# One product of the SSD scan moved from POOL to VectorE, in a hybrid SSD and attention layer

## The chip, the cores and the metric

The kernel runs on one core of a Trainium2 chip, as one program with one launch. The metric is the device time of one execution in microseconds, and a kernel's time is the median over its runs. The profile is one more execution, taken by the hardware profiler. Engine names are those of the profile: PE is TensorE, DVE is VectorE, ACT is ScalarE, POOL is GpSimd and SP is SyncE, which here only issues DMAs.

## The reference

One layer works on 1024 prompt tokens and on 8 streams of 16 tokens, 1152 tokens in all, with a model width of 1024. One input projection feeds two branches, a Mamba-2 scan (the SSD branch: 32 heads of 64 in 8 groups, state width 128) and a forgetting attention (16 heads of 64). The branches are gated, projected back, merged and normalized. What matters here is the chunked scan, cut to its core:

```python
acum = jnp.cumsum(dtc * A, axis=2)
seg = acum[:, :, :, None] - acum[:, :, None]
decay = jnp.exp(jnp.where(causal, seg, -jnp.inf))
cb = jnp.einsum('bclgn,bcsgn->bclsg', Cc, Bc)
m = cb[..., None] * decay * dtc[:, :, None]
y_diag = jnp.einsum('bclsgr,bcsgrp->bclgrp', m, xc)
...
y_off = jnp.einsum('blgn,bgrpn->blgrp', c_c, s_in) * jnp.exp(acum_c)[..., None]
```

For each head and each block of tokens there are two products: `y_diag`, the masked and decayed matrix C·B times the inputs of the block, and `y_off`, C times the state that enters the block, times the decay exp(acum) of each token. The kernel applies that second decay to C ahead of the matmul.

## The kernel before, in words

Everything is fp32. A dense projection splits its inputs and weights into a high and a low part and takes three matmul passes (lines 244 to 246, in `passes`). A weight tile gives 128 output columns for all 1152 tokens, in three column chunks c = 0, 1, 2 of 384 tokens (in chunk 2, 256 tokens are of the prompt and 128 of the streams). Each chunk is 24 matmuls into one PSUM bank, and these products have two banks (tag `d`). So PE starts a chunk's 24 matmuls only when the chunk two before it has been read out of its bank. Who reads it out depends on the column:

- columns of x, B and C (`conv_dense`): ACT copies the bank (L539, in chunk 2 also L545) and starts the convolution (L540). DVE adds the three other taps (L551), ACT takes a tanh (L552) and DVE finishes with L553. The result for C is the tile `acc…c`, `Cf` in the scan.
- columns of the gate z (`silu_dense`): ACT takes a tanh (L569), DVE reads the bank again and multiplies (L570).

Weights are split into parts by ACT and POOL (L223, L224) or, where they have a scale, by ACT and DVE (L226, L227).

The scan runs per group g of four heads. While PE works on the six weight tiles of group g+1 (`group_dense`), a generator `group(g)` is advanced a step at a time by the clock of `passes` (the class `Flow`), so that the scan's small operations are put between the dense matmuls. For each chunk of three token blocks it does this:

- `rows` has SP load, for each head, the running sum acum of the chunk, broadcast to 128 partitions, into a tile `ce`.
- `transp` has PE transpose x and B; DVE multiplies by dt (L612), POOL by the decay to the block's end (L614).
- `cbt` computes C·B and masks it into `cbm` (DVE, L646 and L649).
- `decay`, called twice with two heads each, forms for each head three blocks of exponents `m` from `ce` (DVE, L687), then ACT takes exp of `ce` in place (L689) and of `m` (L690), DVE multiplies `m` by `cbm` (L691), and POOL multiplies `ce` by C in place (L692), 384 columns wide in chunks 0 and 1 and 256 in chunk 2.
- `states` carries the state from block to block (POOL L667, DVE L668).
- `readout` of a chunk, which comes in the next chunk or at the end, has PE multiply with `m` (L708) and with `ce` (L712). DVE adds the skip term (L721), POOL multiplies by the gate (L724), and ACT squares (L727, L729) for the norm, summed by POOL (L730).
- for the streams, POOL decays the states (L751) and DVE adds the updates (L767).

Each engine works through its own queue in order. For this part of the kernel, the order in the queue is not that of the text: the framework's planner orders the operations at compile time, by priority (the order of the text) among those whose inputs its own model has ready. So operations of a later step can stand far ahead of their place in the code. Later parts (attention, merging) have an order written by hand.

Of the kernel before, what the change touches and what calls it, by code (L numbers as in the profile page):

```python
# [15 lines left out]
ALU = mybir.AluOpType  # L16
# [133 lines left out]
def trunk_step(ctx: ExitStack, tc: tile.TileContext, I, O):  # L150
    nc = tc.nc
    ve, ac, po, te, sy = nc.vector, nc.scalar, nc.gpsimd, nc.tensor, nc.sync
# [438 lines left out]
    def group(g, r):  # L591

        sp = lazy["spb"]
        xs, z, Bf, Cf = [r["x0"], r["x1"]], [r["z0"], r["z1"]], r["b"], r["c"]
# [84 lines left out]
        def decay(c, i):  # L679
            w = CW if c < 2 else 256  # L680
            for e in range(2):
                h = 4 * g + 2 * i + e
                m = sp.tile([P, 3, P], F32, tag="m", name=f"m{c}_{h}", bufs=4)
                ce = ces[c, 2 * i + e]
                for j in range(3):
                    b = 3 * c + j
                    ve.tensor_scalar(m[:, j, :], ce[:, j * P:(j + 1) * P], nacum[:, b, h:h + 1], 0.0,  # L687
                                     ALU.add, ALU.min)
                ac.activation(ce[:, :w], ce[:, :w], AF.Exp)  # L689
                ac.activation(m[:], m[:], AF.Exp)  # L690
                ve.tensor_tensor(m[:], m[:], cbms[c][:], ALU.mult)  # L691
                po.tensor_tensor(ce[:, :w], ce[:, :w], Cf[c][:, :w], ALU.mult)  # L692
                mm[c, 2 * i + e] = m

        def readout(c):
# [76 lines left out]
        for c in range(NCH):  # L772
            for j in range(3):
                transp(3 * c + j)
                yield Y
                if c and j == 0:
                    readout(c - 1)
                    yield 2 * Y
            cbt(c)
            yield Y  # L780
            if c == 2:
                stk = stack()
                sample_out()
                yield Y
            decay(c, 0)
            yield Y
            states(c)
            if c == 2:
                for q in range(4):
                    sample_decay(q)  # L790
            yield Y
            decay(c, 1)
            if c < 2:
                for i in range(2):
                    rows(c + 1, i)
            yield Y
# [563 lines left out]
    for c in range(NCH):  # L1360
# [27 lines left out]
        for j in range(3):  # L1388
            b, w = 3 * c + j, width[j]
# [107 lines left out]
```

## Time and profile before

| | us |
|---|---|
| three runs | 2066.13, 2066.86, 2064.82 (median 2066.13) |
| profiled execution | 2064.78 |
| its span, from first to last instruction | 2062.9 |
| scan with the projection of the columns it needs | about 184 to 985 of the span |
| one group in that stage | about 100 |
| busy in the whole span: PE, DVE, ACT, POOL | 2028.5, 1376.8, 820.1, 594.6 |

The lines of a profile that follow below have these forms. A line of the timeline has the start in the span, the duration, the engine, the line of the code, the operation, the tile written and the tiles read, their shapes and how many instructions follow on each other (x3); in brackets stands the idle time of the engine before it, and what ended that. A line of the waits says who waited for whom, with the sum, the number of waits and the longest. A line of the windows says how long an engine was busy in a stretch. A line of one source line has the smallest, the median and the largest duration in ns.

### The profile page before, as it was taken

How to read it: one execution, taken by the hardware profiler on the slowest of the kernel's cores; microseconds unless marked ns; L12 is line 12 of the kernel's file. 1: busy time of each engine (PE TensorE's matmuls, PEld its weight loads, DVE VectorE, ACT ScalarE, POOL GpSimd, SP SyncE). 2: the span in 40 equal slices, each digit the busy share in tenths (PEclk: the TensorE clock that was granted, in tenths of full speed). 3: DMA queues.
4: the chain of work that ended last, by engine and by line, in shares of the span. 5: the costliest groups of instructions: out<-in, count | busy, mean ns of one | idle time of the engine just before them, and what ended most of it. 6: DMA issues, size and time to landing. Idle time of an engine off the chain costs nothing.

```text
span 2062.9 us, 36057 instructions
## 1 busy us (share of the span) xinstructions
PE 2028.5 (98%) x14263; PEld 1868.2 (91%) x14263; DVE 1376.8 (67%) x2278; ACT 820.1 (40%) x1647; POOL 594.6 (29%) x775
## 2 busy tenths in 40 slices
PE   9999999999999999999999999999999999999998
PEld 7899989899998999999988888888889899999987
DVE  4145788887878787874487787777777774173355
ACT  5124444444434344443445554545455452122210
POOL 0013565555556564644100100110010002114400
PEclk9999999999999999999999999999999999999999
DMA  6412242423232323242556566556656584154222
GB/s 221 161 65 90 71 134 71 126 77 119 81 126 78 118 91 114 87 134 91 185 196 194 186 206 207 188 179 199 212 184 202 186 301 147 41 171 152 82 106 92
DMA packets 123624, 292.49 MB, mean 142 GB/s; under 512 B 18632, under 2 KB 74944, under 8 KB 113216
## 3 DMA queue, kind: packets, MB, share of 16 engines
q1 hardware_dynamic: 110912, 208.93, 31.7%
q10 hardware_dynamic: 12544, 81.27, 11.4%
q8 instruction: 112, 1.84, 0.4%
q14 instruction: 56, 0.46, 0.1%
HBM read 233.64 MB, written 56.51 MB: 141 GB/s over the span
## 4 chain that ended last, share of the span: by engine, by line
PE 67%; DVE 20%; ACT 5%; DMA 4%; issue 2%; POOL 1%; ACTq 0%; DVEq 0%; SPq 0%; POOLq 0%
PE d L244 14%; PE d L246 13%; PE d L245 13%; PE s L914 3%; DVE m L687 2%; PE o L989 2%; PE v L333 2%; PE v L334 2%; PE v L332 2%; PE dq L245 2%; PE dq L244 2%; PE dq L246 2%; PE out L1381 2%; PE out L1380 2%; PE out L1382 2%
## 5 line engine op out<-in xcount | busy, mean ns | idle before, releaser
L244 PE MATMUL d<-xh,wh 128*128 128x384 f32 x2112 | 740.9, 351 | 21.3 <-DVE z3z L570 2.1
L246 PE MATMUL d<-xh,wl 128*128 128x384 f32 x2112 | 708.7, 336 | 0.0
L245 PE MATMUL d<-xl,wh 128*128 128x384 f32 x2112 | 707.8, 335 | 0.0
L244 PEld LDWEIGHTS d<-xh,wh 128*128 128x128 f32 x2112 | 397.2, 188 | 54.6 <-issue 17.7
L245 PEld LDWEIGHTS d<-xl,wh 128*128 128x128 f32 x2112 | 397.6, 188 | 0.8
L246 PEld LDWEIGHTS d<-xh,wl 128*128 128x128 f32 x2112 | 396.7, 188 | 0.0
L224 POOL TENSOR_TENSOR wl<-wr,wh 128x1024 fp32r<-128x1024 f32 x52 | 125.5, 2413 | 348.8 <-ACT wh L223 348.8
L687 DVE TENSOR_SCALAR m<-ce,nacum 128x128 f32<-128x128 f32 x288 | 141.6, 553 | 5.9 <-PE y L708 5.9
L223 ACT CAST wh<-wr 128x1024 fp32r<-128x1024 f32 x64 | 67.0, 1047 | 194.9 <-PE d L245 157.1
L919 ACT ACTIVATE st<-s,ckt 128x256 f32<-128x256 f32 (+1 forms) x320 | 115.1, 466 | 20.1 <-PE s L914 14.8
L923 POOL TENSOR_TENSOR st<-st,mask_bf 128x256 f32<-128x256 f32 x64 | 48.3, 775 | 196.8 <-ACT st L919 196.7
L979 ACT ACTIVATE st<-st 128x1024 f32<-128x1024 f32 x80 | 83.1, 1062 | 43.6 <-DVE st L974 41.0
L227 DVE SCALAR_TENSOR_TENSOR wl<-wr,wh 128x1024 fp32r<-128x1024 f32 x50 | 62.2, 1243 | 32.5 <-ACT wh L226 32.1
L614 POOL TENSOR_TENSOR wx<-xdt,wdt 128x256 f32<-128x256 f32 x72 | 56.8, 790 | 50.9 <-DVE xdt L612 50.9
L989 PE MATMUL o<-st,vt 128*64 128x256 f32 (+1 forms) x640 | 69.5, 363 | 1.6 <-ACT st L979 1.2
L989 PEld LDWEIGHTS o<-st,vt 128*64 128x64 f32 x640 | 42.8, 137 | 28.4 <-ACT st L979 5.1
L245 PE MATMUL d<-yb1l,wh 128*128 128x384 f32 x192 | 64.2, 334 | 0.0
L244 PE MATMUL d<-yb1h,wh 128*128 128x384 f32 x192 | 64.2, 334 | 0.0
L246 PE MATMUL d<-yb0h,wl 128*128 128x384 f32 x192 | 64.2, 334 | 0.0
L246 PE MATMUL d<-yb1h,wl 128*128 128x384 f32 x192 | 64.2, 334 | 0.0
L245 PE MATMUL d<-yb0l,wh 128*128 128x384 f32 x192 | 64.2, 334 | 0.0
L244 PE MATMUL d<-yb0h,wh 128*128 128x384 f32 x192 | 64.2, 334 | 0.0
(635 smaller groups left out, 4093.9 us busy)
## 6 DMA issues: line engine op xcount, KB each, us to landing
wr<-in_wt SPq DMA_DIRECT2D x88, 512.0 KB
kc<-in_cache_k ACTq DMA_DIRECT2D x32, 1024.0 KB
vc<-in_cache_v ACTq DMA_DIRECT2D x32, 1024.0 KB
ce<-ac_d SPq DMA_DIRECT2D x96, 192.0 KB
wr<-in_wbr SPq DMA_DIRECT2D x24, 512.0 KB
gate_d<-gate SPq DMA_DIRECT2D x48, 192.0 KB
sb<-cs_d ACTq DMA_DIRECT2D x16, 576.0 KB
yr<-ym_d SPq DMA_DIRECT2D x16, 576.0 KB
```

Of the source, the lines that this page charges most:

```text
L223: ac.copy(hi[:, :cols], raw[:, :cols])
L224: lazy.get("sub", po).tensor_tensor(lo[:, :cols], raw[:, :cols], hi[:, :cols].bitcast(F32), ALU.subtract)
L227: ve.scalar_tensor_tensor(lo[:, :cols], raw[:, :cols], scale, hi[:, :cols].bitcast(F32), ALU.mult, ALU.subtract)
L244: te.matmul(out, wh, xh, start=(k == 0), stop=False)
L245: te.matmul(out, wh, xl, start=False, stop=False)
L246: te.matmul(out, wl, xh, start=False, stop=(k == n - 1))
L614: po.tensor_tensor(wx[b][:], xdt[b][:], wdt[:, b, hs][:, :, None].to_broadcast([P, 4, 64]), ALU.mult)
L687: ve.tensor_scalar(m[:, j, :], ce[:, j * P:(j + 1) * P], nacum[:, b, h:h + 1], 0.0, ALU.add, ALU.min)
L914: te.matmul(ps2[:, e, 256 * x + q0:256 * x + 256], kk[hr, ks], qq[hr, qs], start=(at == 0), stop=(at == 2))
L919: ac.activation(S[j][:, e, kb, q0:], ps2[:, e, 256 * x + q0:256 * x + 256], AF.Identity, bias=ckt[:, kb, 2 * hp + e:2 * hp + e + 1])
L979: ac.activation(w, w, AF.Exp, scale=-1.0)
L989: te.matmul(o[64 * e:64 * e + 64, 256 * at + q0:256 * at + 256], vt[:, kb, 64 * e:64 * e + 64], S[j][:, e, kb, q0:256], start=(kb == 0), s ...
```

## The change

The product of the exponentiated row with C moves from POOL to DVE. In the text it stands behind the product of `m` with the mask, as before.

```diff
                 ac.activation(ce[:, :w], ce[:, :w], AF.Exp)
                 ac.activation(m[:], m[:], AF.Exp)
                 ve.tensor_tensor(m[:], m[:], cbms[c][:], ALU.mult)
-                po.tensor_tensor(ce[:, :w], ce[:, :w], Cf[c][:, :w], ALU.mult)
+                ve.tensor_tensor(ce[:, :w], ce[:, :w], Cf[c][:, :w], ALU.mult)
                 mm[c, 2 * i + e] = m
```

It is executed 96 times: 8 groups, 3 chunks, 4 heads.

## The prediction

> **What bounds the kernel now.** I read the page's first lines, then the busy times in the stage of the scan, then PE's waits in that stage. The first shows PE as the bound of the whole; the second, for PE, DVE, ACT and POOL in that order, leaves PE 805 − 783.0 = 22 us idle between 180 and 985 us; the third says for whom.
>
> ```profile
> span 2062.9 us, 36057 instructions
> PE 2028.5 (98%) x14263; PEld 1868.2 (91%) x14263; DVE 1376.8 (67%) x2278; ACT 820.1 (40%) x1647; POOL 594.6 (29%) x775
> ```
> ```profile
> 180.00:985.00 805.00, 783.03 (x5303) 740.50 (x5302) 630.09 (x1152) 341.87 (x742) 440.55 (x592) 1.00 0.33 103
> ```
> ```profile
> PE d L244 <- DVE z4z L570: 1.8, 2, 1.5
> PE d L244 <- ACT raw4x L545: 1.0, 1, 1.0
> PE d L244 <- ACT raw4c L545: 0.4, 1, 0.4
> ```
>
> The waits are the rows of one group (4); the other groups have rows like them. PE stands still in three places of a group and a little in a fourth, each time for a bank of the dense product that ACT or DVE has not read out yet. So the change can gain at most those 22 us, and it can lose whatever it adds in front of these read-outs. POOL and DVE have idle time, and neither is a bound by its sum. What decides is who stands in front of whom in DVE's and ACT's queues.
>
> The three places, PE's rows first, then ACT's, then DVE's, in the timeline:
>
> ```profile
> 502.32 0.44 PE L244 MATMUL d<-xh,wh 128*128 128x384 f32 x1 [0.38 <-ACT raw3c L545]
> ```
> ```profile
> 535.62 0.45 PE L244 MATMUL d<-xh,wh 128*128 128x384 f32 x1 [1.02 <-ACT raw4x L545]
> ```
> ```profile
> 563.71 0.44 PE L244 MATMUL d<-xh,wh 128*128 128x384 f32 x1 [1.54 <-DVE z4z L570]
> ```
> ```profile
> 499.81 0.53 ACT L552 ACTIVATE raw3c<-acc3c 128x384 f32<-128x384 f32 x1 [3.07 <-DVE acc3c L551]
> ...
> 533.11 0.53 ACT L552 ACTIVATE raw4x<-acc4x 128x384 f32<-128x384 f32 x1 [1.98 <-DVE acc4x L551]
> ...
> 562.17 0.52 ACT L690 ACTIVATE m<-m 128x384 f32<-128x384 f32 x1 [0.61 <-DVE m L687]
> 562.60 0.47 ACT L569 ACTIVATE z4z<-d 128x384 f32<-128x384 f32 x1
> ```
> ```profile
> 494.13 1.26 DVE L687 TENSOR_SCALAR m<-ce,nacum 128x128 f32<-128x128 f32 x2
> 495.31 4.10 DVE L551 SCALAR_TENSOR_TENSOR acc3c<-raw3c,cw,acc3c 128x384 f32<-128x384 f32 x3
> ...
> 522.92 0.61 DVE L721 SCALAR_TENSOR_TENSOR yt<-acc3x,dcol,y 128x384 f32<-128x384 f32 x1
> 523.45 2.24 DVE L687 TENSOR_SCALAR m<-ce,nacum 128x128 f32<-128x128 f32 x3
> ...
> 526.13 3.79 DVE L687 TENSOR_SCALAR m<-ce,nacum 128x128 f32<-128x128 f32 x7
> 529.84 3.18 DVE L551 SCALAR_TENSOR_TENSOR acc4x<-raw4x,cw,acc4x 128x384 f32<-128x384 f32 x3
> ...
> 554.79 0.48 DVE L687 TENSOR_SCALAR m<-ce,nacum 128x128 f32<-128x128 f32 x2
> ...
> 555.71 2.32 DVE L687 TENSOR_SCALAR m<-ce,nacum 128x128 f32<-128x128 f32 x5
> ...
> 558.48 3.60 DVE L687 TENSOR_SCALAR m<-ce,nacum 128x128 f32<-128x128 f32 x5
> ```
>
> I call them the places C, X and Z. At C (502.3) and X (535.6), PE waits for ACT's copy L545; that stands in ACT's queue behind the tanh L552, and the tanh waits for DVE's three L551, which come late. At Z (563.7) the gate's bank is read by ACT L569, which stands behind an exp L690 that waits for DVE's L687. So in all three the late one is DVE, with L687 and L551 in front.
>
> **Why DVE is late there.** These rows are durations of L687 and L692 and the busy time of POOL in the stretches ahead of the three places, first all of POOL, then L692 alone.
>
> ```profile
> L687 DVE TENSOR_SCALAR m<-ce,nacum x288: 272/282/1075, 189.9 to 955.5; 128x128 f32<-128x128 f32 x144
> ...
> L692 POOL TENSOR_TENSOR ce<-ce,acc3c x12: 718/1014/1353, 494.3 to 562.0; 128x384 f32<-128x384 f32 x8, 128x256 f32<-128x256 f32 x4
> ```
> ```profile
> 494.00:499.50 5.50, 4.70 (x6) 1.00 0.59 215
> 522.50:533.10 10.60, 7.75 (x9) 1.00 0.37 113
> 554.70:562.00 7.30, 5.25 (x7) 1.00 0.32 115
> ```
> ```profile
> 494.00:499.50 5.50, 4.28 (x4) 1.00 0.59 215
> 522.50:533.10 10.60, 4.67 (x4) 1.00 0.37 113
> 554.70:562.00 7.30, 2.41 (x4) 1.00 0.32 115
> ```
>
> An L687 takes 0.28 us, and two in a row 0.48, so 0.20 for each further one. The longest takes 1.075, about as long as a product L692 of POOL (1.014). So a DVE operation on SBUF seems to stand still for as long as a POOL operation is running, not merely to go slower. The Trainium skill (SBUF — State Buffer, "SBUF: two separate sides") says the same: the port pair that DVE and POOL share is an exclusive lock, and the loser is blocked for the whole instruction. With an even split of the port 0.28 would have become 0.56, not 1.075; by a split the relief below would be half, and the sum 3.1 us a group slower, 2086. The trace agrees with the lock.
>
> **Removed: POOL's product, and what it blocks.** Free of POOL, three L551 take 0.61 + 2 × 0.53 = 1.67 us, by these rows (the start of the next operation is 0.53 behind that of L551):
>
> ```profile
> 492.39 0.61 DVE L551 SCALAR_TENSOR_TENSOR acc3c<-raw3c,cw,acc3c 128x384 f32<-128x384 f32 x1
> 492.92 0.68 DVE L767 TENSOR_TENSOR s<-s,up 128x512 f32<-128x512 f32 x1
> ```
>
> At each place I take DVE's time above its free time, times L692's share of POOL's busy time.
> C: (1.26 − 0.48) + (4.10 − 1.67) = 3.21; share 4.28/4.70; 2.92 us.
> X: L687 (2.24 − 0.68) + (3.79 − 1.48) = 3.87, L551 3.18 − 1.67 = 1.51, sum 5.38; share 4.67/7.75; 3.24 us.
> Z: (2.32 − 1.08) + (3.60 − 1.08) = 3.76; share 2.41/5.25; 1.73 us.
> That is 7.9 us of a group of DVE's time. Nothing on POOL waits for the freed time: its queue there is L538, L614, L724, L730, which are released by ACT and DVE, and POOL is idle for 805 − 440.6 us.
>
> **Added: the product on DVE.** The nearest row is DVE's other product with two operands in SBUF; four take 1.97 us, so 0.55 + 3 × 0.47. For 256 columns the nearest is the mask product, 0.33 from start to start:
>
> ```profile
> 510.07 1.97 DVE L691 TENSOR_TENSOR m<-m,cbm 128x384 f32<-128x384 f32 x4
> ...
> 567.09 0.42 DVE L646 TENSOR_TENSOR cbm<-cb,cst 128x256 f32<-128x256 f32 x1
> 567.42 0.28 DVE L649 TENSOR_TENSOR cbm<-cb,cst 128x128 f32<-128x128 f32 x1
> ```
>
> So a group gets 8 × 0.47 + 4 × 0.33 = 5.1 us, less than the 7.9 it is relieved of. Where do they stand? The order in a queue is not that of the text: POOL's first L692 of this group started at 494.3, sixteen us before the group's first L691 (510.07), which the text has ahead of it. So I expect DVE's L692 early too, close behind its exp L689, among the L687 and L551 of the three places: 4 × 0.47 = 1.88 at C and X, 4 × 0.33 = 1.32 at Z. Their readers have time: L721, which follows the readout, starts at 522.92, some 11 us after the L691 of that chunk.
>
> **Added: a wait.** L692 waits for ACT's L689, and this one for DVE's three L687, since it overwrites their input. On POOL that wait held up only POOL; on DVE it holds L687, L551 and L570 behind it.
>
> ```profile
> POOL ce L692 <- ACT ce L689: 31.4, 23, 2.7
> ...
> ACT ce L689 <- DVE m L687: 41.5, 47, 3.6
> ```
> ```profile
> 533.67 0.56 DVE L553 SCALAR_TENSOR_TENSOR acc4x<-raw4x,acc4x 128x384 f32<-128x384 f32 x1 [0.65 <-ACT raw4x L552]
> ```
>
> POOL had 23 such waits, one at each place nearly (24 places in 8 groups). What DVE pays when it waits for one ACT operation that follows it directly is 0.65 (L553). The price of a place lies between nothing (other operations stand between) and four such waits, 2.6; I take one, 0.65, by POOL's count.
>
> **The sum.** C: −2.92 + 1.88 + 0.65 = −0.39, which covers the stall of 0.38. X: −3.24 + 1.88 + 0.65 = −0.71 of a stall of 1.02. Z: −1.73 + 1.32 + 0.65 = +0.24, a loss. Per group 0.38 + 0.71 − 0.24 = 0.85 us, and in the seven groups that have dense work of a next group beside them 6 us. The profiled execution took 2064.8 (span 2062.9 and 1.9 around it), so 2058.8, rounded 2059; the median of the runs, 2066.1, is 1.3 above that execution. With no wait the three places give 0.38 + 1.02 + 0.41 = 1.81, 12.7 us, 2052. With two each (1.3) C loses 0.26, X gains 0.06 and Z loses 0.89: 7.6 us slower, 2072.
>
> **Rivals.**
> The products go elsewhere. If the planner puts L692 behind L691, as the text has it, the three places get all of the relief (2.92, 3.24 and 1.73, over 0.38, 1.02 and 1.54) and nothing added; DVE idles around L691's places. All 22 us go: 2043. For it speaks the text, against it where POOL had L692. Chance 0.17.
> The wait takes over. DVE stands behind ACT's exp more than once at a place: break-even lies near 1.4 waits a place, two give 2072, four give (1.56 + 1.24 + 2.19) × 7 = 35 us, 2100. For it speaks that each L692 has its own exp and that ACT's queue holds operations which wait for POOL and DVE in turn; against it, that twelve L687 are there to stand between. Chance 0.25.
> The change moves nothing that PE sees: relief and addition are eaten by other waits, for DVE also waits for L724 and L730, which stay on POOL. 2061 to 2069. Chance 0.18.
>
> **How the numbers follow.** My own case has 0.40, of which 0.33 end faster by over 0.2% (4.1 us, about what a measurement can tell from nothing here) and 0.07 within. Faster 0.33 + 0.17 = 0.50; within 0.07 + 0.18 = 0.25; slower 0.25. The range goes from 2045, near all stalls gone, to 2076, a little over two waits a place.
>
> **What would show it.** Right: POOL's 95.7 us of L692 gone (12 of them in a group), L687's mean falling from about 0.55 towards 0.4, the L551 at C back at about 0.6, PE's idle time in the stage at about 16 us, C's row gone and X's halved. Wrong: DVE rows of L692 with idle time before them that ACT L689 ended, and longer waits of PE for L570; or L692 standing behind L691, with all PE waits gone.
>
> ```profile
> 180.00:985.00 805.00, 95.66 (x96) 1.00 0.33 103
> ...
> L687 DVE TENSOR_SCALAR m<-ce,nacum 128x128 f32<-128x128 f32 x36 | 17.7, 555 | 0.0
> ```

## The result and the profile after

The change makes the kernel faster by far more than forecast: 2035.5 us (median of 4 runs, 2034.5 to 2036.1) against 2066.5 (4 runs), a ratio of 0.985 with an interval of 0.983 to 0.987, 31 us. The direction was right. The size was not: the forecast was 2059, and 2035.5 lies below the range and even below the 2043 that the prediction named as the least that the change could reach. All times here are medians of executions at a granted clock of 0.998 to 1.000; one execution of e1 had a clock of 0.85, took 2203.1 us and is left out.

The profiled execution's span went from 2062.9 to 2033.8 us, 29.1 less. All of it is in the scan: from the first start of L612 to the last it takes 755.9 us before (201.7 to 957.6) and 726.8 after (200.8 to 927.6). The page's first lines after the change, and the busy times between 180 and 985 us (PE, weight loads PEld, DVE, ACT, POOL):

```profile
span 2033.8 us, 36030 instructions
PE 2020.1 (99%) x14263; PEld 1866.5 (92%) x14263; DVE 1355.8 (67%) x2374; ACT 817.8 (40%) x1647; POOL 508.2 (25%) x679
```
```profile
180.00:985.00 805.00, 805.00 (x5509) 768.37 (x5508) 617.54 (x1260) 352.10 (x770) 355.23 (x500) 1.00 0.35 111
```

In the whole execution DVE got 96 more operations and is busy for 21.0 us less (1376.8 to 1355.8). (The stretch from 180 to 985 us holds more of the work after the change, since the kernel gets further in it; busy times in it can't be subtracted from those of before.) PE's matmuls leave no idle time at all in the stage. That is the 22 us of the prediction's bound, but the time went down by 29, and PE cannot save idle time that it did not have. The weight loads show the rest. The page's line for them, of before and then of after, with the idle time ahead of them behind the second bar:

```profile
L244 PEld LDWEIGHTS d<-xh,wh 128*128 128x128 f32 x2112 | 397.2, 188 | 54.6 <-issue 17.7
```
```profile
L244 PEld LDWEIGHTS d<-xh,wh 128*128 128x128 f32 x2112 | 396.9, 188 | 26.0 <-issue 16.5
```

That is 28.6 us less, nearly all of the 29.1. The same waits of group 4 as the prediction read from the matmuls, now from the weight loads, before:

```profile
PEld d L244 <- DVE z4z L570: 2.3, 2, 1.9
...
PEld d L244 <- ACT raw4x L545: 1.2, 1, 1.2
PEld d L244 <- ACT raw4c L545: 0.6, 1, 0.6
...
PEld d L244 <- ACT acc4x L540: 0.2, 1, 0.2
```

and all that is left of them after:

```profile
PEld d L244 <- ACT raw4x L552: 0.2, 1, 0.2
```

So group 4 lost 4.3 us (2.3 + 1.2 + 0.6 + 0.2), not the 3.2 of the matmul rows, and 0.2 is left. C's row is smaller in some groups (0.2 to 0.6); over all groups these rows sum to 29.3 us before and 1.6 after. (The row raw4c is place C one group on; at 502.3 us its name is raw3c, also 0.6.)

DVE at the three places after the change, C, X and Z:

```profile
482.52 0.28 DVE L687 TENSOR_SCALAR m<-ce,nacum 128x128 f32<-128x128 f32 x1
482.71 1.02 DVE L692 TENSOR_TENSOR ce<-ce,acc3c 128x384 f32<-128x384 f32 x2
483.65 0.61 DVE L551 SCALAR_TENSOR_TENSOR acc3c<-raw3c,cw,acc3c 128x384 f32<-128x384 f32 x1
484.18 0.55 DVE L692 TENSOR_TENSOR ce<-ce,acc3c 128x384 f32<-128x384 f32 x1
...
485.37 0.61 DVE L551 SCALAR_TENSOR_TENSOR acc3c<-raw3c,cw,acc3c 128x384 f32<-128x384 f32 x1
486.05 0.56 DVE L692 TENSOR_TENSOR ce<-ce,acc3c 128x384 f32<-128x384 f32 x1
```
```profile
510.64 1.46 DVE L687 TENSOR_SCALAR m<-ce,nacum 128x128 f32<-128x128 f32 x3
...
512.55 0.55 DVE L692 TENSOR_TENSOR ce<-ce,acc3c 128x384 f32<-128x384 f32 x1
513.02 2.96 DVE L687 TENSOR_SCALAR m<-ce,nacum 128x128 f32<-128x128 f32 x7
...
517.90 0.60 DVE L551 SCALAR_TENSOR_TENSOR acc4x<-raw4x,cw,acc4x 128x384 f32<-128x384 f32 x1
518.43 0.55 DVE L692 TENSOR_TENSOR ce<-ce,acc3c 128x384 f32<-128x384 f32 x1
```
```profile
539.52 0.48 DVE L687 TENSOR_SCALAR m<-ce,nacum 128x128 f32<-128x128 f32 x2
...
544.03 2.01 DVE L687 TENSOR_SCALAR m<-ce,nacum 128x128 f32<-128x128 f32 x6
545.96 0.79 DVE L692 TENSOR_TENSOR ce<-ce,acc3c 128x256 f32<-128x256 f32 x2
...
547.12 0.56 DVE L570 SCALAR_TENSOR_TENSOR z4z<-z4z,d 128x384 f32<-128x384 f32 x1
```

The products stand where the prediction put them, early, between the L687 and L551. No bracket with idle time stands before any of them, and in the whole trace the idle time ahead of the 96 products is 0.5 us. And L551 takes its free 0.6 us again, the L687 in the rows with several in a row 2.96 for seven where it was 3.79.

### The profile page after: what moved, and what is told of

Its sections match the earlier page's. It is cut to its first block, busy times and chain, and to the rows that moved or that the text cites. A ratio compares the mean times of both kernels' runs of the same rounds, so it can differ in the third digit from the quotient of the medians.

```text
span 2033.8 us, 36030 instructions
## 1 busy us (share of the span) xinstructions
PE 2020.1 (99%) x14263; PEld 1866.5 (92%) x14263; DVE 1355.8 (67%) x2374; ACT 817.8 (40%) x1647; POOL 508.2 (25%) x679
## 4 chain that ended last, share of the span: by engine, by line
PE 90%; DVE 5%; DMA 4%; ACT 1%; issue 1%; POOL 0%; SPq 0%; ACTq 0%; DVEq 0%
PE d L244 20%; PE d L246 19%; PE d L245 19%; PE s L914 3%; PE y L708 2%; PE o L989 2%; PE dq L246 2%; PE dq L245 2%; PE dq L244 2%; PE out L1382 2%; PE out L1380 2%; PE out L1381 2%; PE v L333 2%; PE v L334 2%; PE v L332 2%; DVE st L974 2%
## 5 line engine op out<-in xcount | busy, mean ns | idle before, releaser
L224 POOL TENSOR_TENSOR wl<-wr,wh 128x1024 fp32r<-128x1024 f32 x52 | 125.5, 2413 | 374.6 <-ACT wh L223 374.6
L687 DVE TENSOR_SCALAR m<-ce,nacum 128x128 f32<-128x128 f32 x288 | 105.7, 421 | 6.1 <-PE y L708 5.9
L227 DVE SCALAR_TENSOR_TENSOR wl<-wr,wh 128x1024 fp32r<-128x1024 f32 x50 | 62.0, 1240 | 30.8 <-ACT wh L226 30.8
L614 POOL TENSOR_TENSOR wx<-xdt,wdt 128x256 f32<-128x256 f32 x72 | 59.0, 820 | 73.7 <-DVE xdt L612 73.7
L689 ACT ACTIVATE ce<-ce 128x384 f32<-128x384 f32 (+1 forms) x96 | 46.5, 484 | 44.8 <-DVE m L687 44.5
```

Of the source, the lines that this page charges most:

```text
L224: lazy.get("sub", po).tensor_tensor(lo[:, :cols], raw[:, :cols], hi[:, :cols].bitcast(F32), ALU.subtract)
L227: ve.scalar_tensor_tensor(lo[:, :cols], raw[:, :cols], scale, hi[:, :cols].bitcast(F32), ALU.mult, ALU.subtract)
L614: po.tensor_tensor(wx[b][:], xdt[b][:], wdt[:, b, hs][:, :, None].to_broadcast([P, 4, 64]), ALU.mult)
```

## The experiments

**Theory 1**: POOL's product blocks DVE on their shared way into SBUF. That made DVE late at the read-outs of PE's banks, and taking the work off POOL is what gains. **Rival 2**: the planner made new orders for the queues of DVE and ACT, and the new order is what gains. **Rival 3**, which came up on the way: what counts is that POOL's queue is shorter, so that the operations behind the product run earlier. For the runs that put work back on POOL (e2, e3, e6, e7, e8) the queues of PE, DVE and ACT have, operation for operation, the order of the changed kernel.

| run | what POOL does for each product | us | ratio to before, interval |
|---|---|---|---|
| after | nothing | 2035.5 | 0.985 (0.983 to 0.987) |
| e1 | nothing, and DVE nothing either | 2034.9 | 0.985 (0.983 to 0.987) |
| e2 | four short reading operations, 2 us | 2072.6 | 1.003 (1.002 to 1.005) |
| e3 | six memsets, 1.5 us | 2052.6 | 0.993 (0.992 to 0.995) |
| e6 | two short reading operations, 1 us | 2047.9 | 0.991 (0.990 to 0.993) |
| e7 | four memsets, 1 us | 2043.7 | 0.989 (0.988 to 0.991) |
| e8 | one long reading operation, 1 us | 2071.1 | 1.002 (1.001 to 1.003) |

### e1: no product on either engine

```diff
-                ve.tensor_tensor(ce[:, :w], ce[:, :w], Cf[c][:, :w], ALU.mult)
```

> Leaves out the product of the decays with C on both engines, so the readout uses the plain decays. The queues of PE and DVE have the same order as in the kernel before, ACT's nearly so. Theory 1 (POOL's product blocks DVE on the shared SBUF port, and that made DVE late): with POOL's product gone PE's waits for ACT and DVE in the scan go as they did after the change, 2030 to 2040 us, although no queue was reordered. Rival 2 (the new order of the DVE and ACT queues is what freed PE): the old order keeps the old waits, 2058 to 2068 us.

Measured 2034.9 us, the same as after the change and in theory 1's range. DVE's queue has the old order here, without a single difference, and ACT's has eight operations at other places. So no new order is needed for the gain, which speaks against rival 2. And the product costs nothing on DVE that PE sees: leaving out DVE's 5 us a group gains no further. In this run the L551 of the kind that stands at C takes its free 0.61 again, and an L687 0.42 in the mean:

```profile
L687 DVE TENSOR_SCALAR m<-ce,nacum 128x128 f32<-128x128 f32 x288 | 104.1, 423 | 5.9 <-PE y L707 5.9
...
L551 DVE SCALAR_TENSOR_TENSOR acc3c<-raw3c,cw,acc3c 128x384 f32<-128x384 f32 x6 | 3.7, 613 | 0.1
```

Before, the same two lines had 553 and 977 ns.

### e2 and e3: POOL given work back, first try

```diff
                 ve.tensor_tensor(ce[:, :w], ce[:, :w], Cf[c][:, :w], ALU.mult)
+                dm = sp.tile([P, 64], F32, tag="dm", name=f"dm{c}_{h}", bufs=1)
+                for k in range(4 if c < 2 else 3):
+                    ks = slice(64 * k, 64 * k + 64)
+                    po.tensor_tensor(dm[:], ce[:, ks], Cf[c][:, ks], ALU.mult)
```

> The changed kernel, with POOL given back about 1 us of work behind each of DVE's products: four (three in chunk 2) products of 64 columns of ce and C into a scratch tile that nobody reads. DVE's and ACT's queues have the same order as after the change. Theory 1: POOL reads SBUF again for as long as before, so DVE is blocked again and has its own products on top: PE's waits come back, 2055 to 2085 us. Rival 2 (order): 2033 to 2038 us.

```diff
                 ve.tensor_tensor(ce[:, :w], ce[:, :w], Cf[c][:, :w], ALU.mult)
+                dm = sp.tile([P, 64], F32, tag="dm", name=f"dm{c}_{h}", bufs=1)
+                po.tensor_copy(dm[:, 0:3], ce[:, 0:3])
+                for _ in range(6):
+                    po.memset(dm[:], 0.0)
```

> As e2, but POOL's extra work is one copy of 3 columns and six memsets of 64 columns, about 1 us that writes SBUF and reads nearly nothing. Same order of DVE's and ACT's queues as after. Theory 1a (any POOL operation holds the port): as e2, 2055 to 2085 us, and L551 and L687 both far above their free 0.61 and 0.28 us. Theory 1b (only an operation that reads blocks DVE's two-input operations): L551 stays at 0.61, L687 may still be blocked, 2035 to 2050 us. Rival 2 (order): 2033 to 2038 us.

Measured 2072.6 and 2052.6 us: e2 in theory 1's range, e3 between the ranges of 1b and 1a. The order alone would have kept both near 2035, so rival 2 is out. But neither tells the lock from the queue. The short operations took longer than meant: sixteen of e2's took 8.15 us, 2 us for each product instead of one, and a memset with the pause behind it 0.21. So POOL was busier than before the change (467.5 and 439.1 us from the first L687 to the last, against 424.6). And DVE was hardly blocked: in the same stretch, which holds the same operations, it is busy for 600.9 us in e2 and 591.7 in e3, against 590.2 after the change. So e2 met theory 1's range mostly for another reason, and in e3 PE waited although DVE was not held up: something else was pushed back. That was the reason for e6 to e8.

### e6, e7 and e8: the same time on POOL in three forms

e6 is e2 with two products instead of four, e7 is e3 with four memsets instead of six. e8 has one operation of full width:

```diff
                 ve.tensor_tensor(ce[:, :w], ce[:, :w], Cf[c][:, :w], ALU.mult)
+                cv = ce[:, :w].rearrange("p (a b) -> p a b", a=32)
+                po.tensor_tensor(cv, cv, ones[:, :, None].to_broadcast([P, 32, w // 32]), ALU.mult)
```

> As e2, with two products of 64 columns in place of four, so that POOL is given about 1 us of reading work for each product, as much as the change took away. PE's, DVE's and ACT's queues have the order of after. Lock of reading operations: DVE is blocked for part of it, 2048 to 2066 us. Order alone: 2033 to 2038 us. Length of POOL's queue alone: the same as the next run, e7.

> As e3, with four memsets in place of six, about 1 us for each product, so that POOL's queue is no longer than before the change. PE's, DVE's and ACT's queues have the order of after. Lock of reading operations alone: memsets do not block, 2034 to 2040 us. Length of POOL's queue: part of e3's loss stays, 2040 to 2050 us, the same as e6.

> As e6, but POOL's extra work is one long operation: behind DVE's product, POOL multiplies the same 384 (256) columns in place by a tile of ones, about 1 us that reads SBUF throughout, as the product did before the change. PE's, DVE's and ACT's queues have the order of after. If DVE stands still for the whole of a POOL operation that reads, one long operation costs more than two short ones: L687 and L551 go back to up to 1.1 and 1.4 us, and with DVE's own 5 us a group on top the time is 2056 to 2080 us. If what counts is only the length of POOL's queue: 2042 to 2050 us, as in e6 and e7.

POOL is now busy for the same time in all three as in the kernel before. The busy times (PE, PEld, DVE, ACT, POOL) from the first start of L687 to the last, which holds the same operations in each run, after the change and in e6, e7 and e8; before the change POOL has 424.6 us there:

```profile
190.70:925.00 734.30, 734.30 (x5035) 701.31 (x5033) 590.20 (x1213) 327.35 (x717) 338.30 (x474) 1.00 0.34 107
```
```profile
190.30:935.80 745.50, 738.30 (x5041) 703.05 (x5040) 603.33 (x1214) 326.77 (x718) 422.90 (x662) 1.00 0.33 105
```
```profile
190.50:932.30 741.80, 735.62 (x5035) 702.04 (x5033) 591.48 (x1214) 325.24 (x717) 422.40 (x944) 1.00 0.34 106
```
```profile
190.30:962.60 772.30, 743.38 (x5044) 703.52 (x5043) 636.95 (x1214) 328.76 (x718) 426.08 (x568) 1.00 0.32 101
```

The times are 2047.9, 2043.7 and 2071.1 us. e8 takes back all of the gain and some more; DVE is busy for 47 us more than after (637.0 against 590.2) with the same operations in the same order, and for 13 and 1 more in e6 and e7. In e8 at place C, DVE first, then POOL:

```profile
498.19 1.20 DVE L551 SCALAR_TENSOR_TENSOR acc3c<-raw3c,cw,acc3c 128x384 f32<-128x384 f32 x1
499.31 1.20 DVE L692 TENSOR_TENSOR ce<-ce,acc3c 128x384 f32<-128x384 f32 x1
500.43 0.60 DVE L551 SCALAR_TENSOR_TENSOR acc3c<-raw3c,cw,acc3c 128x384 f32<-128x384 f32 x1
```
```profile
497.88 2.21 POOL L694 TENSOR_TENSOR ce<-ce,ones 128x384 f32<-128x384 f32 x2 [0.66 <-DVE ce L692]
500.59 1.16 POOL L694 TENSOR_TENSOR ce<-ce,ones 128x384 f32<-128x384 f32 x1 [0.50 <-DVE ce L692]
```

While POOL's two long operations run (497.88 to 500.09), L551 and L692 take 1.20 us each, for 0.6 and 0.55 alone. So theory 1 holds: same orders, same time on POOL, and of the three forms only the one long operation that reads brings the whole loss back. None of PE's waits in e8 is for POOL, so it is not that the readout had to wait for POOL's product. Two short operations (e6) let DVE in between them: at the same place in e6, POOL first,

```profile
487.28 5.00 POOL L696 TENSOR_TENSOR dm<-ce,acc3c 128x64 f32<-128x64 f32 x8 [0.66 <-DVE ce L692]
```
```profile
488.19 0.67 DVE L692 TENSOR_TENSOR ce<-ce,acc3c 128x384 f32<-128x384 f32 x1
```

Rival 3 has a part too. e7's memsets do not hold DVE up, and yet e7 is 8 us slower than after, above the 2034 to 2040 of the lock alone; and e6 is 4 us slower than e7, where the length of POOL's queue alone would have made them the same. The reason for e7's loss is in these rows of it, POOL, DVE and the weight loads:

```profile
491.03 0.78 POOL L696 MEMSET dm<- 128x64 f32 x4
491.78 2.39 POOL L224 TENSOR_TENSOR wl<-wr,wh 128x1024 fp32r<-128x1024 f32 x1
```
```profile
491.95 2.50 DVE L551 SCALAR_TENSOR_TENSOR acc3c<-raw3c,cw,acc3c 128x256 f32<-128x256 f32 x1 [0.95 <-ACT acc3c L540]
```
```profile
498.45 0.19 PEld L244 LDWEIGHTS d<-xh,wh 128*128 128x128 f32 x1 [1.13 <-DVE z4z L570]
```

The weight split L224 is queued behind the memsets, starts just ahead of the next chunk's L551 and blocks it for nearly all of its 2.4 us. After the change L224 starts by itself at 487.87, and that L551 (488.73) takes 1.81. Behind this L551 stand ACT's tanh L552 and L569 and DVE's L570, for which PE waits 1.1 us; six groups have such a wait, and after the change none has. So an operation on POOL can cost DVE in two ways: by what it blocks itself and by where it pushes the next one that blocks.

### e4: one chunk's products at a time

```diff
-                ve.tensor_tensor(ce[:, :w], ce[:, :w], Cf[c][:, :w], ALU.mult)
+                (ve if c == 1 else po).tensor_tensor(ce[:, :w], ce[:, :w], Cf[c][:, :w], ALU.mult)
```

and the same with `c == 0` and `c == 2`.

> Only chunk 0's products are on DVE, those of chunks 1 and 2 stay on POOL. By the weight loads' waits of before, place C (0.62 us a group) and the gate's small wait behind it (0.41) go, X and Z stay: about 7 us, 2059 us. With chunk 1's 17.7 us and chunk 2's the parts should add up to the 31 us of the whole change, if they do not hide each other.

> Only chunk 1's products (a third of them) are on DVE, those of chunks 0 and 2 stay on POOL. Theory of the prediction (each place by itself): only place X and the small wait behind it gain, 1.4 us a group by the weight loads' rows, 10 us, about 2056 us. Theory of carried lateness (DVE's backlog at X is still there at Z): Z's wait shrinks too by about 1 us a group, about 2049 us.

> Only chunk 2's products are on DVE, those of chunks 0 and 1 stay on POOL. The run with chunk 1 alone left 0.85 us a group at place Z; that part belongs to chunk 2's products, so about 6 us, 2060 us. By the prediction's step for Z (relief 1.73, added 1.32, one wait of 0.65) it would be no gain, 2066 to 2068 us.

Measured: chunk 0 alone 2058.7 us (ratio 0.996, 0.995 to 0.998), chunk 1 alone 2048.5 (0.991, 0.990 to 0.993), chunk 2 alone 2060.3 (0.997, 0.996 to 0.998). Against the runs of before beside them (2066.1, 2066.2 and 2066.1) that is 7.4, 17.7 and 5.8 us, in sum 30.9, the whole gain: the parts add up. Chunk 1 came out as carried lateness had it (2049), not as each place by itself (2056). Chunk 1's products are at place X, but they are worth more than X's 1.2 us a group. The waits of group 4 with chunk 1 alone:

```profile
PEld d L244 <- DVE z4z L570: 1.3, 2, 0.8
...
PEld d L244 <- ACT raw3c L545: 0.6, 1, 0.6
```

X's row is gone, C's is as before, and Z's longest wait went from 1.9 to 0.8, although chunk 2's products, which stand at Z, are still on POOL. From the first L687 at Z to the read-out L570 DVE takes 8.31 us in both runs (554.79 to 563.10 before, 545.16 to 553.47 here); it only gets there earlier. So DVE's lateness at X is carried on to Z. Chunk 2's products alone take Z's longest wait from 1.9 to 1.2.

### e5: the gate's product moved as well

```diff
-            po.tensor_tensor(zc, zc, yt[:], ALU.mult)
+            ve.tensor_tensor(zc, zc, yt[:], ALU.mult)
```

> The changed kernel with the multiplication by the gate (L724, 48 operations, which still block DVE for some 34 us) moved to DVE too. If PE is now the bound of the scan, with some 5 us of waits for other engines left in the whole stage, the time stays within 3 us of the changed kernel's 2035.5; if the lock still costs PE something that the waits do not show, it is faster by more than that; if DVE's load is near its limit, slower.

Measured 2034.7 us (ratio to before 0.984, 0.982 to 0.986), the same as the changed kernel. L724 still blocks DVE after the change, but only 0.2 us a group of PE's waits for late read-outs is left, so next to nothing is to be had there. PE sets the time of this stage now.

## Why the prediction was wrong

**What bounds the kernel.** Right that PE is the bound and that it waits for late read-outs; wrong in "So the change can gain at most those 22 us". The matmul rows end 0.33 us after they start while one starts every 0.17, so a stop of PE reads short by the part that overlaps, and short stops do not show. At Z the matmul's row said 1.54 us; the weight load's row at the same moment says 1.86:

```profile
563.71 0.19 PEld L244 LDWEIGHTS d<-xh,wh 128*128 128x128 f32 x1 [1.86 <-DVE z4z L570]
```

By the weight loads the limit was the 29.3 us of their rows, 2064.8 − 29.3 = 2035.5; the profiled execution after the change took 2035.6. The line with 54.6 us idle stood on the page of before. The Trainium skill has a rule near this (Perfetto Trace Analysis, "Identifying the Most-Contended Engine"): for how close a kernel is to roofline (the most that the engine could do), matmul busy time is a poor measure since matmuls are pipelined, and the share of the weight loads a better one. The trace agrees in that the matmul rows hide idle time: in the stage before the change PE is 783.0 us busy by the matmuls and 740.5 by the weight loads.

**Why DVE is late.** Right, and shown by e8 against e6 and e7: DVE stands still while a long POOL operation that reads SBUF runs (L551 and L692 1.20 us in e8 for 0.6 and 0.55 alone).

**Removed.** The relief was estimated at 7.9 us a group, the addition at 5.1, so DVE should have 2.8 us a group less, 22 in all. From the first L687 to the last, DVE's busy time fell from 612.3 to 590.2 us, by 22. That the two agree so well is partly luck: some products meet L724, which stays on POOL (1.25 us at 542.85, where 0.42 is free), so group 4's took about 6.0 us from start to start and not 5.1, and the relief must have been larger by as much.

**Added: the product.** Right in place, and in size where it meets no POOL operation: 0.47 from start to start (1.02 for two), among L687 and L551. It does not stand wholly ahead of the read-outs: at C and X one of the four comes after the last L551.

**Added: a wait.** This step failed. I took one wait of 0.65 us for ACT's exp at each place, from POOL's 23 waits. There was none: DVE stood idle for 0.5 us ahead of all 96 products together. The planner put other work between an exp and its product, and DVE, unlike POOL, was busy enough never to arrive early. POOL's waits said how idle POOL was, not what DVE would pay.

**The sum.** This failed in two more steps: the stops that could be gained were read too short (above), and the places were taken one by one. The forecast was 0.85 us a group, and 4.1 us of waits went in group 4 (4.3 less the 0.2 that is left). Of the 3.2 between them, the price of the wait makes 1.0 (0.31 at X, 0.65 at Z). The true length of the three stops (0.2, 0.2 and 0.3 more) and the gate's second wait of 0.4, which the prediction left out, make 1.1. The rest, 1.1, is at Z: without the wait my terms gave 0.41 there, and the whole stop went. e4 shows where this comes from: chunk 1's products, at X, take 1.0 us off the wait at Z. DVE from the first L687 to the read-out L570 at Z is only 0.7 us shorter (554.79 to 563.10 before, 539.52 to 547.12 after); it also starts earlier.

**The rivals.** The products did not move behind L691, DVE did not wait for ACT's exp ahead of them, and PE's waits went, so none of the three was what happened. The time fell below the 2043 of the first by another way. Two of the signs that were named came as named: L687's mean fell from 0.55 to 0.42 us, and the L551 at C took 0.61 us.

## What to carry to other kernels

Read PE's idle time from the weight loads, not from the matmuls; their waits give the limit of what a change on another engine can gain. A long operation on POOL that reads SBUF can cost DVE up to about its own length where the two meet; e8's 96 of about 1 us cost 47 us, half their length in the mean. So a product that takes 1.0 us on POOL and 0.55 on DVE can be cheaper for DVE when DVE does it. An engine that is late at one place can still be late at the next (here 1.0 us from X to Z), so take the places of a queue together, and price a wait from the engine that will do the waiting. To compare busy times, take stretches that hold the same operations: a fixed stretch of time holds more work of the faster kernel.

## What the runs showed of the hardware that was not expected

Blocking goes both ways. After the change, where DVE's L227 (1.21 us, two inputs in SBUF) and L553 behind it are running, POOL's L614 takes 2.00 us instead of about 0.6 (0.62 at 547.17):

```profile
519.24 1.21 DVE L227 SCALAR_TENSOR_TENSOR wl<-wr,wh 128x1024 fp32r<-128x1024 f32 x1
```
```profile
519.39 2.00 POOL L614 TENSOR_TENSOR wx<-xdt,wdt 128x256 f32<-128x256 f32 x1 [3.69 <-DVE xdt L612]
```

Memsets on POOL do not block DVE's operations with two inputs. In e7, four memsets run on POOL from 487.06 and four from 488.59, and L692 and L551 have their free durations in that time:

```profile
487.40 0.55 DVE L692 TENSOR_TENSOR ce<-ce,acc3c 128x384 f32<-128x384 f32 x1
487.87 0.61 DVE L551 SCALAR_TENSOR_TENSOR acc3c<-raw3c,cw,acc3c 128x384 f32<-128x384 f32 x1
488.40 0.28 DVE L687 TENSOR_SCALAR m<-ce,nacum 128x128 f32<-128x128 f32 x1
488.60 0.61 DVE L551 SCALAR_TENSOR_TENSOR acc3c<-raw3c,cw,acc3c 128x384 f32<-128x384 f32 x1
```
```profile
487.06 0.78 POOL L696 MEMSET dm<- 128x64 f32 x4
487.91 0.62 POOL L694 COPY dm<-ce 128x3 f32<-128x3 f32 x1
488.59 0.81 POOL L696 MEMSET dm<- 128x64 f32 x4
```

The Trainium skill (SBUF — State Buffer, "Who interferes with whom") has two-input operations of DVE contend only with a POOL operation that reads SBUF; these rows agree.

L687, with one tensor from SBUF, is another matter. It keeps its free duration beside the memsets too, but there the memsets take longer: four of them 0.97 us instead of 0.78 beside a row of L687 in e7.

```profile
547.59 0.97 POOL L696 MEMSET dm<- 128x64 f32 x4
```
```profile
546.45 2.02 DVE L687 TENSOR_SCALAR m<-ce,nacum 128x128 f32<-128x128 f32 x6
```

Single memsets go up to 0.31 us beside L687 and stay at 0.15 beside L551 and L692. So L687 and a memset do seem to keep each other out; whether a longer memset would hold L687 up no run here shows.
